# First mixer: 31-tap convolution moved to TensorE strips; first expert stage: pipeline in a written-out order, overflow branch at its head

## The chip, the cores and the metric

One Trainium2 chip, one of its cores. The kernel is one launch. The metric is device time in microseconds (us) of that launch. Beside it stands a profile of one execution, with a trace of every instruction: TensorE (PE, and PEld for its weight loads), VectorE (DVE), ScalarE (ACT), GpSimd (POOL) and SyncE's DMA queue (SP).

## The reference, cut to what matters

Two layers over 256 latent and 256 context tokens of 1024 channels. The parts that this change touches:

```python
def conformer_conv(p, dw_w, dw_b, ln_g, ln_b):
    v, g = jnp.split(p, 2, -1)
    u = v * jax.nn.sigmoid(g)
    u = depthwise_conv(u, dw_w, PAD_A) + dw_b          # 31 taps along the tokens, 512 channels
    return jax.nn.silu(layer_norm(u, ln_g, ln_b))

def moe(h, router_w, router_bias, w_gate, w_up, w_down):   # 16 experts, each token goes to two
    ...
    for e in range(N_EXPERTS):
        hid = jax.nn.silu(t @ w_gate[e]) * (t @ w_up[e])
        out = out + combine[:, e:e + 1] * (hid @ w_down[e])
    return out.reshape(shp)
```

The first layer's mixer runs `conformer_conv` beside a bidirectional gated recurrence (RG-LRU) and one output projection; both layers end in `moe`, the first over 512 tokens, the second over the 256 latent tokens.

## The kernel before

All matrix products keep fp32 accuracy by splitting each operand into a rounded part and its rest (`hi`, `lo`, both fp32r) and adding three products. A weight arrives from DRAM as a 1 MB tile `raw` (SP issues it), is split in two halves by ACT (line 138, `hi`) and DVE or POOL (line 140, `lo`) into a pair of `hl` tiles, and is used by PE. `Feeder` keeps that going: `load` issues transfers into free tiles, `one` splits one half, `get` hands out the next pair. There are four pairs; three `raw` tiles always, and more (`rawx`, `rawy`) in the expert stages.

The order of instructions on an engine is set by a scheduler that follows dependencies and priorities, except inside `in_order()`, where the order of the program text is the order on PE, ACT, DVE and POOL.

**First mixer** (lines 560 to 815). Channels lie on partitions, four groups g of 128; tokens run along the free axis, both segments side by side (512 columns). `value_gate(g)` projects the value and gate columns and writes the gated product into the padded buffer `ups` (line 607). The depthwise convolution goes by `taps`: for every one of 31 taps one instruction over 128x512 multiplies by the channel's weight and adds into `u2` (line 625 on DVE, lines 622 and 623 on POOL). Group 3 is POOL's, groups 2, 1 and 15 taps of group 0 are DVE's, and 16 taps of group 0 are PE's with a diagonal matrix for each tap (`taps_pe`, line 639). Between them stand the recurrence's small convolution (`ub` to `vl`, lines 661 to 668), its gates on PE (line 680), coefficients and scans, the projections for `gg`, and the modulation products with the conditioning vector (`ada_fill`; line 350: four products of 128x32 by 512 columns in the four column strips of the array). A layer norm over channels follows; its first product is line 906, after which `u2` is centred (line 913).

**First expert stage** (`moe`, lines 1121 to 1310). For each expert, a matrix `pm` picks its up to 128 tokens; an indirect DMA on POOL gathers them (`xg`, line 1144), PE transposes them (line 1165), ACT and DVE split them into `xT`. Then gate and up (24 products of 128x128 by 512 columns each, line 1177), `silu(gate)*up` (lines 1240 and 1242), four transposes (1245), a split (1246, 1247), down (24 products, line 1271), a weighted copy into `y` (1276 on ACT, 1277 on DVE) and a scatter to `YD` on POOL (1157). The last two experts are not scattered but combined by products with a placing matrix (line 1305). Before expert 14 stands `overflow` (line 1015): a branch that is taken only when more than 128 tokens chose one expert. There too the rows of `YD` are read back, and four weight tiles (`HOLD`) are held back until then. The second expert stage (`moe_latent`) is written inside `in_order()` and is not changed.

Of the kernel before, what the change touches and what calls it, by code (L numbers as in the profile page):

```python
# [14 lines left out]
D = 1024  # L15
# [32 lines left out]
HOLD = 4  # L48
# [120 lines left out]
def _body(tc, nc, pool, psum, dram, a):  # L169
# [89 lines left out]
    V.memset(PRb[:, :128], 0.0)  # L259

    def late_params():
# [9 lines left out]
        Q.dma_start(PRb[:124, 128:256], a["a_dw_w"].rearrange("o t (k p) -> (o t k) p", p=128))  # L271
        Q.dma_start(PRb[:12, 256:384], a["c_conv_w"].rearrange("o t (k p) -> (o t k) p", p=128))
# [139 lines left out]
    DWT = pool.tile([128, 136], F32, name="DWT")  # L412
# [112 lines left out]
    for g in (2, 1):  # L525
        vg_unit(g)
    half_unit(2)
    vg_unit(0)
# [26 lines left out]
    T.transpose(pp[:, 128:252], PRb[:124, 128:256], ident[:124, :124])  # L555
    T.transpose(pp[:, 252:264], PRb[:12, 256:384], ident[:12, :12])
    V.tensor_copy(PRT[:, 48:128], pp[:, :80])
    V.tensor_copy(DWT, pp[:, 128:264])
    cmR, PR_ = open_pool("mix0_right", "right")
    feed.ada = (PR_, RAWM0)  # L560
# [38 lines left out]
    ups_ = [ups[:, 576 * g:576 * g + 572].rearrange("p (s t) -> p s t", s=2) for g in range(4)]  # L599
# [12 lines left out]
    def taps(g, eng, ts):  # L612

        dst = seg(u2[:, 512 * g:512 * g + 512])
        for t in ts:
            w = DWT[:, 4 * t + g:4 * t + g + 1]
            src = ups_[g][:, :, t:t + 256]
            if t == 0:
                ins = eng.tensor_scalar(dst, src, w, param("a_dw_b", g), OP.mult, OP.add)
            elif eng is G:  # L620
                m_ = seg(PR_.tile([128, 512], F32, name="cm", tag="cm", bufs=1))
                G.tensor_tensor(m_, src, w.unsqueeze(2).broadcast_to([128, 2, 256]), OP.mult)
                ins = G.tensor_tensor(dst, dst, m_, OP.add)
            else:
                ins = V.scalar_tensor_tensor(dst, src, w, dst, OP.mult, OP.add)  # L625
        if len(ts):
            mark(f"conv{g}", ins)

    def taps_pe(g, ts):
        pt = bank()  # L630
        diag = PR_.tile([128, 2048], F32, name="diag", tag="iv", bufs=1)
        for n, t in enumerate(ts):
            d_ = diag[:, 128 * n:128 * n + 128]
            w = DWT[:, 4 * t + g:4 * t + g + 1]
            if DIAG(n):
                S.activation(d_, ident, AF.Copy, scale=w)
            else:
                G.tensor_tensor(d_, ident, w.broadcast_to([128, 128]), OP.mult)
            T.matmul(seg(pt), d_, ups_[g][:, :, t:t + 256], start=n == 0, stop=n == len(ts) - 1)
        return pt  # L640
# [66 lines left out]
    def lru(d):  # L707
        if d:
            load_gates(1)
        lru_gates(d)  # L710
        lru_coeff(d)
        lru_scan(d)

    feed.pool_lo = PL_S
    lru(0)
    value_gate(0)
    lru(1)
    gg = PR_.tile([128, 2048], F32, name="gg", tag="vl", bufs=1)
    for g in range(4):
        pt = proj(nT, feed.get())  # L720
        S.activation(gg[:, 512 * g:512 * g + 512], pt, AF.Gelu_apprx_tanh)
        ada_fill(ADA_E)
    def row_bc(A, third, j0, r, nh):
# [12 lines left out]
    def add_experts(layer, u0, u1):  # L736
        us = []
        for e in range(NE):
            units = []
            for nm in ("moe_w_gate", "moe_w_up"):  # L740
                w = a[nm][layer, e].rearrange("(p k) f -> p k f", p=128)
                units += [(w[:, k0:k0 + 4], 512) for k0 in (0, 4)]
            w = a["moe_w_down"][layer, e].rearrange("(p k) n -> p k n", p=128)
            units += [(w[:, k0:k0 + 2], 1024) for k0 in (0, 2)]
            us += units
        for u in us[u0:u1]:
            feed.add(*u)
# [44 lines left out]

    taps(3, G, range(31))
    taps(0, G, range(POOL_TAPS))
    for g in (2, 1):
        taps(g, V, range(31))
# [6 lines left out]
    pt = taps_pe(0, range(31 - PE_TAPS, 31))  # L803
    taps(0, V, range(POOL_TAPS, 31 - PE_TAPS))
    dst = seg(u2[:, :512])
    V.tensor_tensor(dst, dst, seg(pt), OP.add)
# [315 lines left out]
    def moe(layer, nt, pl, before_tail=None):  # L1122
# [28 lines left out]
        def dispatch(e):  # L1151
            pd = pick(e, slots(e), 0, 8)
            gather(e, pd)
            weight(e, pd)

# [14 lines left out]
        def unit(out_, s, wp, k0, m, last):  # L1170
            hi, lo = wp
            for k in range(2):
# [3 lines left out]
                for l, r_ in ((xh, wh), (xh, wl), (xl, wh)):  # L1176
                    ins = T.matmul(out_, l, r_, start=m == 0, stop=m == last)  # L1177
                    if m == 0:
                        mark("e%d" % e, ins)
# [8 lines left out]
        for e in range(2):  # L1188
            first.append(slots(e))
            gather(e, pick(e, first[e], 0, 4))  # L1190
            if e == 1:

                V.tensor_scalar(one, disp[:, 1, 0:1], 0.0, 1.0, OP.mult, OP.add)
                feed.gate, feed.boost = one, GBOOST
                feed.split()
                feed.gate, feed.boost = None, BOOST
# [20 lines left out]
        s = xT(0)  # L1217
        for e in range(NE):
            if e == NE - 4:
                zero = pl.tile([128, D], F32, name="zero", tag="y", bufs=3)  # L1220
                G.memset(zero, 0.0)
            if e == NE - 2:

                overflow(layer, nt, pl, posm)
                yss = [feed.raw_tile(True) for _ in range(nt)]
                for i in range(nt):
                    Q.dma_start(yss[i], YD[256 * i:256 * i + 256].rearrange("(p t) d -> p (t d)", t=2))
                add_experts(layer, 6 * NE - HOLD, 6 * NE)
                feed.load()
            pgu = []  # L1230
            for _ in range(2):
                pb = bank()
                pgu.append(pb)
                m = 0
                for k0 in (0, 2, 4, 6):
                    m = unit(pb, s, feed.get(), k0, m, 23)
            if e < NE - 1:
                sn = xT(e + 1)
            sl_ = tmp()
            S.activation(sl_, pgu[0], AF.Silu)  # L1240
            hd = tmp()
            V.tensor_tensor(hd, sl_, pgu[1], OP.mult)
# [5 lines left out]
            if e + 2 < NE:  # L1248
                dispatch(e + 2)
                if e + 2 >= NE - 2:  # L1250
                    scatter(e + 2, zero)
            if e == NE - 1:
                gbs = [pl.tile([128, D], F32, name="gb", tag="xg", bufs=2) for _ in range(nt // 2)]
                for r in range(nt // 2):
                    for nh in range(2):
                        S.activation(gbs[r][:, 512 * nh:512 * nh + 512], row_bc(A, 2, 2, r, nh), AF.Copy)
                for i in range(nt):
                    ys = yss[i]
                    G.tensor_tensor(ys[:, :D], ys[:, :D], ys[:, D:], OP.add)
# [653 lines left out]
```

## Time and profile before

| | |
|---|---|
| median of 3 runs | 1280.6 us (1279.28 to 1281.32) |
| the profiled execution's own time | 1279.8 us |
| its span, first to last instruction | 1278.1 us |
| PE busy | 1099.0 us, 86% |
| DVE busy | 991.4 us, 78% |
| ACT busy | 718.4 us, 56% |
| POOL busy | 459.5 us, 36% |
| mean granted TensorE clock | 0.940 |
| moved by DMA | 303.46 MB, 237 GB/s |

Busy time is a sum over stages that differ. The span falls into: norm and modulation (to 58), first mixer (58 to 236), its output projection and routing (236 to 324), first expert stage (324 to 678), second mixer (to about 870) and second expert stage (to the end).

### The profile page before, as it was taken

To read this page: it belongs to the slowest core of one execution; us is meant where nothing else is said; L and a number is where in the kernel's file an instruction comes from. 1 tells how busy PE (TensorE), PEld (TensorE's weight loads), DVE (VectorE), ACT (ScalarE), POOL (GpSimd) and SP (SyncE) were. 2 spreads that over 40 slices of the span, in tenths; PEclk is the share of its full clock that TensorE was granted. 3 is DMA by queue.
4 is the path that set the end of the run, shared out by engine and by line. 5 is a ranking of instruction groups with operands and counts; after the bars stand their busy time and mean duration, and the time that the engine had idled before them with its cause. 6 is when DMAs were issued, how large, how long until landed. Compare 5 with 4: busy or idle time off the path is not lost. (4 is left out here: it accounts for less than half of the span.)

```text
span 1278.1 us, 15407 instructions
## 1 busy us (share of the span) xinstructions
PE 1099.0 (86%) x5370; PEld 823.1 (64%) x5371; DVE 991.4 (78%) x1210; ACT 718.4 (56%) x962; POOL 459.5 (36%) x393
## 2 busy tenths in 40 slices
PE   5896479897799999999888999996699888898975
PEld 3664245585577777777666866665577677776763
DVE  3369999856799999898895335775988888879983
ACT  4321455423577777777664234452578667768781
POOL 3299912444111121212414500023345445545551
PEclk9898689998799999999997999998899999999997
DMA  9772217431699989999595477732678877878840
GB/s 302 233 253 93 82 66 282 193 119 66 254 313 330 344 315 332 332 362 331 198 361 183 150 265 271 256 149 82 202 262 295 295 279 268 298 268 312 288 180 33
DMA packets 94063, 303.46 MB, mean 237 GB/s; under 512 B 14930, under 2 KB 56161, under 8 KB 64792
## 3 DMA queue, kind: packets, MB, share of 16 engines
q1 hardware_dynamic: 89160, 293.38, 64.8%
q0 software_dynamic: 4816, 9.00, 2.2%
q8 instruction: 45, 0.74, 0.2%
q14 instruction: 42, 0.34, 0.1%
HBM read 299.15 MB, written 11.60 MB: 243 GB/s over the span
## 5 line engine op out<-in xcount | busy, mean ns | idle before, releaser
L140 DVE TENSOR_TENSOR hl<-rawx,hl 128x1024 fp32r<-128x1024 f32 x163 | 226.5, 1396 | 28.3 <-ACT hl L138 24.5
L140 DVE TENSOR_TENSOR hl<-raw,hl 128x1024 fp32r<-128x1024 f32 x128 | 175.5, 1380 | 68.4 <-ACT hl L138 50.0
L138 ACT ACTIVATE hl<-rawx 128x1024 fp32r<-128x1024 f32 x174 | 182.3, 1059 | 66.1 <-PE psa L1271 22.9
L138 ACT ACTIVATE hl<-raw 128x1024 fp32r<-128x1024 f32 x142 | 148.7, 1057 | 123.2 <-PE psb L453 30.9
L1509 PE MATMUL psa<-hl,xT 128*128 128x512 f32 x432 | 118.6, 422 | 21.3 <-DVE xT L1589 17.1
L1509 PE MATMUL psa<-hlx,xT 128*128 128x512 f32 x432 | 116.9, 417 | 12.4 <-DVE xT L1589 10.2
L1509 PEld LDWEIGHTS psa<-hl,xT 128*128 128x128 f32 x432 | 85.1, 201 | 45.2 <-DVE xT L1589 12.9
L1509 PEld LDWEIGHTS psa<-hlx,xT 128*128 128x128 f32 x432 | 84.4, 200 | 36.2 <-DVE xT L1589 9.1
L1144 POOL DMA_INDIRECT xg<-XN,dispi x16 | 29.4, 1840 | 192.2 <-DVE pm L1131 168.3
L1177 PE MATMUL psb<-hl,xT 128*128 128x512 f32 x384 | 93.9, 400 | 0.4 <-PEq L1017 0.4
L1271 PE MATMUL psb<-hl,xT 128*128 128x512 f32 x192 | 81.1, 422 | 13.6 <-ACT xT L1246 9.6
L1177 PE MATMUL psa<-hl,xT 128*128 128x512 f32 x384 | 92.2, 396 | 0.0
L1177 PEld LDWEIGHTS psb<-hl,xT 128*128 128x128 f32 x384 | 72.6, 190 | 18.6 <-issue 0.8
L1177 PEld LDWEIGHTS psa<-hl,xT 128*128 128x128 f32 x384 | 72.1, 188 | 17.5
L1271 PE MATMUL psa<-hl,xT 128*128 128x512 f32 x192 | 78.0, 406 | 2.9 <-DVE xT L1247 2.2
L453 PE MATMUL psb<-nT,hl 128*128 128x512 f32 x288 | 76.6, 413 | 0.1
L625 DVE SCALAR_TENSOR_TENSOR u<-ups,DWT,u 128x512 f32<-128x512 f32 x74 | 76.2, 1071 | 0.2
L453 PEld LDWEIGHTS psb<-nT,hl 128*128 128x128 f32 x288 | 55.1, 195 | 20.7 <-issue 5.6
L140 DVE TENSOR_TENSOR hlx<-rawx,hlx 128x1024 fp32r<-128x1024 f32 x38 | 59.9, 1586 | 7.5 <-ACT hlx L138 7.3
L140 POOL TENSOR_TENSOR hlx<-rawx,hlx 128x1024 fp32r<-128x1024 f32 x18 | 49.2, 2733 | 45.6 <-ACT hlx L138 40.8
L140 POOL TENSOR_TENSOR hl<-raw,hl 128x1024 fp32r<-128x1024 f32 x14 | 38.0, 2716 | 62.5 <-ACT hl L138 60.3
L140 POOL TENSOR_TENSOR hl<-rawx,hl 128x1024 fp32r<-128x1024 f32 x17 | 45.4, 2671 | 39.5 <-ACT hl L138 32.3
(501 smaller groups left out, 2335.9 us busy)
## 6 DMA issues: line engine op xcount, KB each, us to landing
rawx<-in_moe_w_down_dram SPq DMA_DIRECT2D x40, 1024.0 KB
rawx<-in_moe_w_gate_dram SPq DMA_DIRECT2D x39, 1024.0 KB
rawx<-in_moe_w_up_dram SPq DMA_DIRECT2D x37, 1024.0 KB
raw<-in_ada_w_dram SPq DMA_DIRECT2D x24, 1024.0 KB
raw<-in_moe_w_up_dram SPq DMA_DIRECT2D x24, 1024.0 KB
raw<-in_moe_w_gate_dram SPq DMA_DIRECT2D x23, 1024.0 KB
raw<-in_moe_w_down_dram SPq DMA_DIRECT2D x20, 1024.0 KB
rawx<-in_ada_w_dram SPq DMA_DIRECT2D x16, 1024.0 KB
```

What stands on the lines that cost most here:

```text
L138: nc.scalar.activation(h3, src, AF.Copy, scale=1.0 if self.gate is None else self.gate)
L140: (nc.gpsimd if self.pool_lo and self.ns % self.pool_lo == 0 else nc.vector).tensor_tensor(l3, src, h3.bitcast(F32), OP.subtract)
L453: ins = T.matmul(pt, l, r, start=k == 0 and m == 0, stop=k == 7 and m == 2)
L625: ins = V.scalar_tensor_tensor(dst, src, w, dst, OP.mult, OP.add)
L1144: G.indirect_dma_start(out=xgs[e % 2], out_offset=None, in_=XN, in_offset=bass.IndirectOffsetOnAxis(ap=dispi[:, e, 1:2], axis=0), bounds_c ...
L1177: ins = T.matmul(out_, l, r_, start=m == 0, stop=m == last)
L1271: T.matmul(pb, l, w_[:, 512 * nh:512 * nh + 512], start=m == 0, stop=m == 11)
L1509: ins = T.matmul(po, l, w_[:, c0:c0 + 512], start=k == 0 and m == 0, stop=k == n * per - 1 and m == len(mm) - 1)
```

## The change

**Convolution.** `taps` and `taps_pe` go. `pack(g)` makes a tile `cz` in which partition 32j+c holds channel c of a strip of 32 channels shifted by j tokens, for the four strips of group g: 16 transfers from `ups`, issued by POOL. `conv(g)` builds two weight tiles on POOL and runs 8 times 4 products (K = 4 taps x 32 channels, 32 columns out, 512 tokens), one for each strip of the array; ACT adds the bias on the way to `u2`. There is one `cz` buffer. `value_gate`, `lru_gates`, `lru_coeff` and `lru_scan` are written in another order, the weight tiles likewise, and the separate tile for the modulation weights (`rawm`) goes, so these share the three `raw` tiles.

**First expert stage.** It runs inside `in_order()`: up of expert e+1 stands between gate and down of expert e, split into halves around the four transposes; the transposes for `xT` of expert e+2 come after down; splits (`split()`) are placed by hand between the products; both halves of `y` are ACT's. The overflow branch moves ahead of the first split tiles. `HOLD` is 0. The read-back of `YD` comes after expert 14, and its additions are placed among expert 15's products.

```diff
@@ first mixer
-    feed.ada = (PR_, RAWM0)
+    zs = {}
+    def pack(g):
+        z = zs[g] = PR_.tile([128, 4, 2, 288], F32, name="cz", tag="cz", bufs=1)
+        for G4 in range(4):
+            for j in range(4):
+                G.dma_start(z[32 * j:32 * j + 32, G4, :, :284], ups_[g][32 * G4:32 * G4 + 32, :, j:j + 284])
+    def conv(g):
+        ws = []
+        for h in range(2):
+            ws.append(tmp().rearrange("p (q G c) -> p q G c", q=8, c=32))
+            G.tensor_tensor(ws[-1], gsum.unsqueeze(1).unsqueeze(1).broadcast_to([128, 8, 2, 32]),
...
+        for q in range(8):
+            for G4 in range(4):
+                T.matmul(seg(pt[32 * G4:32 * G4 + 32]), ws[G4 // 2][:, q, G4 % 2], zs[g][:, G4, :, 4 * q:4 * q + 256],
+                         start=q == 0, stop=q == 7)
+        S.activation(u2[:, 512 * g:512 * g + 512], pt, AF.Identity, bias=param("a_dw_b", g))
...
     value_gate(3, early.pts)
-    for g in (2, 1):
-        value_gate(g)
+    pack(3)
     for g in range(4):
         pt = proj(nT, feed.get())
         if g == 0:
             load_gates(0)
+        if g == 2:
+            conv(3)
...
-    lru(0)
+    lru_gates(0)
+    value_gate(2)
+    pack(2)
+    lru_coeff(0)
+    value_gate(1)
+    conv(2)
+    pack(1)
+    lru_scan(0)
+    load_gates(1)
+    lru_gates(1)
     value_gate(0)
-    lru(1)
+    conv(1)
+    pack(0)
+    lru_coeff(1)
+    lru_scan(1)
...
-    taps(3, G, range(31))
-    taps(0, G, range(POOL_TAPS))
-    for g in (2, 1):
-        taps(g, V, range(31))
...
-    pt = taps_pe(0, range(31 - PE_TAPS, 31))
-    taps(0, V, range(POOL_TAPS, 31 - PE_TAPS))
@@ first expert stage
+        overflow(layer, nt, pl, posm)
+        V.tensor_scalar(one, disp[:, 1, 0:1], 0.0, 1.0, OP.mult, OP.add)
+        feed.gate, feed.boost = one, GBOOST
+        feed.split()
...
+        def expert(e):
+            s = ops[e]
+            if e + 2 < NE:
+                pms[e + 2] = slots(e + 2)
+            pg, m = bank(), 0
+            for k0 in (0, 2, 4, 6):
+                m = product(pg, e, k0, m)
+                if k0 < 6:
+                    split()
+                    rest(1)
...
+            if e + 1 < NE:
+                pu, m = bank(), 0
+                for k0 in (0, 2):
+                    m = product(pu, e + 1, k0, m)
+                    split()
             ph = bank()
             for k in range(4):
                 T.transpose(ph[:, 128 * k:128 * k + 128], hd[:, k::4], ident)
...
+                for k0 in (4, 6):
+                    m = product(pu, e + 1, k0, m)
+                    split()
...
-                V.tensor_scalar(y[:, 512:], pd1, w_, None, OP.mult)
+                S.activation(y[:, 512:], pd1, AF.Copy, scale=w_)
                 scatter(e, y)
...
+            split()
+            if e + 2 < NE:
+                ops[e + 2] = xT(e + 2)
```

What this does to the order on the engines, at the places that the prediction speaks of.

PE, second half of the first mixer, before (`nT,hl` projections, `vl,gw` gates of the recurrence, `condT` modulation, `ups,diag` taps, `Am` the broadcast of gates ahead of line 906):

```order
L453 MATMUL psb<-nT,hl 128x512 x16
L639 MATMUL psa<-ups,diag 128x512 x2
L350 MATMUL psa<-raw,condT 32x512 x4
L639 MATMUL psa<-ups,diag 128x512 x3
L350 MATMUL psa<-rawm,condT 32x512 x4
L639 MATMUL psa<-ups,diag 128x512 x11
L727 MATMUL psb<-Am_92,ident 128x512
```

and PE with the change, from the end of `value_gate(1)` to the start of `conv(0)` (`cz,tmp` are the strips):

```order
L353 MATMUL psa<-raw,condT 32x512 x4
L678 MATMUL psb<-vl,gw 128x512 x4
L456 MATMUL psb<-nT,hl 128x512 x5
L635 MATMUL psa<-cz,tmp 32x512 x3
L678 MATMUL psa<-vl,gw 128x512
L635 MATMUL psa<-cz,tmp 32x512 x29
L678 MATMUL psa<-vl,gw 128x512 x3
L456 MATMUL psb<-nT,hl 128x512 x19
L353 MATMUL psa<-raw,condT 32x512 x4
L456 MATMUL psa<-nT,hl 128x512 x24
L353 MATMUL psa<-raw,condT 32x512 x4
L456 MATMUL psa<-nT,hl 128x512 x3
```

The taps on PE, which stood at the end, are replaced by four blocks of 32 strip products that stand among projections and gates; the next row after this piece is the first strip product of `conv(1)`.

POOL in the same stretch, with the change, from the end of the recurrence's constants (`NSP`) to the sums for the layer norm (line 902):

```order
L585 TENSOR_SCALAR NSP_480<-w_481 128x8
L622 DMA cz<-ups 32x2x284 x16
L629 TENSOR_TENSOR tmp<-gsum,DWT 128x512 x2
L622 DMA cz<-ups 32x2x284 x16
L629 TENSOR_TENSOR tmp<-gsum,DWT 128x512 x4
L902 TENSOR_TENSOR tmp<-u_513 128x512
L622 DMA cz<-ups 32x2x284 x16
L902 TENSOR_TENSOR tmp<-tmp,u_513 128x512 x2
```

Before, 30 pairs of a multiply and an add over 128x512 stood here; now there are the packs of groups 2, 1 and 0, the last one behind a layer-norm sum. The pack of group 3 stands ahead, mixed one to one with the small instructions of the recurrence's constants.

PE, an expert in the middle of the first expert stage, with the change (`pm` the pick for expert e+2, `ident,tmp` the four transposes):

```order
L1157 MATMUL psb<-ident,xg 128x128 x4
L1157 MATMUL psa<-ident,xg 128x128 x4
L1169 MATMUL psb<-hl,xT 128x512 x24
L1135 LDWEIGHTS pm
L1135 MATMUL psa<-RM,pm 128x8
```

```order
L1135 MATMUL psa<-RM,pm 128x8
L1169 MATMUL psb<-hl,xT 128x512 x12
L1251 MATMUL psa<-ident,tmp 128x128 x4
L1169 MATMUL psb<-hl,xT 128x512 x12
L1266 MATMUL psb<-hl,xT 128x512
```

The first piece is gate of expert e, with the operand of the expert after it just before; the second is up of expert e+1, cut in half by the transposes of expert e, and then down of expert e. Before, gate and up of one expert stood together, and the transposes and down followed them with nothing between.

## Rows read from the trace of the kernel before

**Rows 1.** Busy time by stretch; columns as in the second line.

```profile
core 0: us, PE busy (x) PEld busy (x) DVE busy (x) ACT busy (x) POOL busy (x), PEclk, DMA share, GB/s
58.50:236.00 177.50, 139.58 (x538) 80.90 (x537) 162.12 (x163) 70.78 (x102) 114.48 (x98) 0.88 0.42 148
...
352.73:597.96 245.23, 228.41 (x1057) 181.60 (x1056) 220.78 (x253) 182.96 (x205) 41.20 (x26) 1.00 0.93 334
...
928.00:1216.00 288.00, 257.24 (x1295) 210.72 (x1294) 250.18 (x222) 207.72 (x250) 141.92 (x52) 0.97 0.81 285
```

**Rows 2.** Groups by line, 58.5 to 236: busy, mean ns | idle before, releasers.

```profile
L625 DVE SCALAR_TENSOR_TENSOR u<-ups,DWT,u 128x512 f32<-128x512 f32 x74 | 76.2, 1071 | 0.2
...
L680 PE MATMUL psb<-vl,gw 128*128 128x512 f32 x16 | 12.5, 876 | 32.8 <-DVE vl L668 26.8 <-DVE ups L607 5.4 <-PE psa L453 0.6
```

**Rows 3.** Timeline of PE, first mixer: start, us, instruction [idle before <-releaser].

```profile
70.58 1.06 PE L350 MATMUL psa<-raw,condT 128*32 128x512 f32 x8
...
94.70 5.76 PE L453 MATMUL psa<-nT,hl 128*128 128x512 f32 x24
100.30 5.76 PE L453 MATMUL psb<-nT,hl 128*128 128x512 f32 x24
...
124.99 2.04 PE L680 MATMUL psb<-vl,gw 128*128 128x512 f32 x2 [10.80 <-DVE vl L668]
...
168.49 1.02 PE L680 MATMUL psb<-vl,gw 128*128 128x512 f32 x2
...
236.26 1.55 PE L906 MATMUL psb<-tmp,onesm 128*128 128x512 f32 x2 [2.64 <-POOL tmp L905]
```

**Rows 4.** Timeline of DVE, the centring of the layer norm.

```profile
240.04 2.47 DVE L913 TENSOR_TENSOR u<-u,psb 128x512 f32<-128x512 f32 x4
```

**Rows 5.** Timelines of POOL, and of DVE at 471.40: transfers that POOL issues, a split beside one.

```profile
344.17 0.99 POOL L1144 DMA_INDIRECT xg<-XN,dispi  x1 [21.98 <-DVE pm L1131]
...
471.40 1.23 DVE L140 TENSOR_TENSOR hl<-raw,hl 128x1024 fp32r<-128x1024 f32 x1
...
471.54 1.98 POOL L1144 DMA_INDIRECT xg<-XN,dispi  x1 [13.30 <-DVE pm L1131]
...
705.28 0.68 POOL L1689 DMA_DIRECT2D tmp<-in_d_rpb_dram  x1
...
709.55 0.55 POOL L1691 DMA_DIRECT2D RP<-tmp  x1 [0.34 <-DVE tmp L1690]
```

**Rows 6.** DMA issues: size, median us from issue to landing.

```profile
RP<-tmp POOLq DMA_DIRECT2D x1, 60.0 KB, 1.9
```

**Rows 7.** Timeline of ACT, first mixer: the one wait for a weight tile.

```profile
83.12 1.06 ACT L138 ACTIVATE hl<-raw 128x1024 fp32r<-128x1024 f32 x1 [2.64 <-DMA raw<-in_ab_w_in_dram]
```

**Rows 8.** Timeline of PE, an expert in the middle of the first stage.

```profile
385.92 0.74 PE L1245 MATMUL psb<-ident,tmp 128*128 128x128 f32 x4 [0.41 <-DVE tmp L1242]
387.35 0.50 PE L1271 MATMUL psb<-hl,xT 128*128 128x512 f32 x1 [0.69 <-ACT xT L1246]
...
388.85 0.50 PE L1271 MATMUL psb<-hl,xT 128*128 128x512 f32 x1 [0.31 <-DVE xT L1247]
```

**Rows 9.** Timeline of PE, start and end of the first expert stage.

```profile
324.00 1.12 PE L1165 MATMUL psb<-ident,xg 128*128 128x128 f32 x4 [3.48 <-DMA xg<-XN,dispi]
...
636.58 0.80 PE L1271 MATMUL psa<-hl,xT 128*128 128x512 f32 x1 [2.20 <-DVE xT L1247]
...
663.89 0.63 PE L1305 MATMUL psb<-yy,tmp 128*128 128x512 f32 x2
...
671.22 0.79 PE L1305 MATMUL psa<-yy,tmp 128*128 128x512 f32 x1 [2.19 <-DVE yt L1288]
...
678.29 1.07 PE L425 MATMUL psb<-rawx,condT 128*32 128x256 f32 x16
```

**Rows 10.** Timeline of PE, the first products after each overflow branch.

```profile
618.92 5.84 PE L1177 MATMUL psb<-hl,xT 128*128 128x512 f32 x24 [0.37 <-PEq L1017]
...
1244.45 3.75 PE L1509 MATMUL psa<-hl,xT 128*128 128x512 f32 x8 [3.88 <-DVEq L1017]
```

More of the change, by code (lines that the diff above doesn't have):

```diff
@@ L47 @@
 RP_POS = 1
-HOLD = 4
+HOLD = 0
 ADA_PRE = 3
@@ L610, in _body @@
     u2 = PW.tile([128, 2048], F32, name="u2", tag="u2", bufs=1)
[L612 to L627, printed above, removed]
@@ L722, in _body @@
         ada_fill(ADA_E)
+        if g == 1:
+            conv(0)
     def row_bc(A, third, j0, r, nh):
@@ L736, in add_experts @@
     def add_experts(layer, u0, u1):
+        parts = [("up", 0)]
+        for e in range(NE):
+            parts += [("gate", e)] + [("up", e + 1)] * (e + 1 < NE) + [("down", e)]
         us = []
[L738 to L745, printed above, removed]
+        for part, e in parts:
+            w = a["moe_w_" + part][layer, e].rearrange("(p k) f -> p k f", p=128)
+            step = 2 if part == "down" else 4
+            us += [(w[:, k0:k0 + step], 2048 // step) for k0 in (0, step)]
         for u in us[u0:u1]:
@@ L1216, in moe @@
             weight(e, pick(e, first[e], 4, 8))
[L1217 to L1242, printed above, removed]
+        overflow(layer, nt, pl, posm)
@@ new lines, in moe, with split, rest, product @@
+        V.tensor_scalar(one, disp[:, 1, 0:1], 0.0, 1.0, OP.mult, OP.add)
+        feed.gate, feed.boost = one, GBOOST
+        feed.split()
+        feed.gate, feed.boost = None, BOOST
+        feed.ahead = 1
+        ops, pus, pms = {}, {}, {}
+        later = deque()
+        def split(n=1):
+            for _ in range(n):
+                feed.one()
+        def rest(n):
+            for _ in range(n):
+                if later:
+                    later.popleft()()
+        def product(pb, e, k0, m):
+            return unit(pb, ops[e], feed.get(), k0, m, 23)
@@ L1272, in moe @@
                     m += 1
+                if kk < 3:
+                    split()
+                    rest(2)
+            rest(99)
             w_ = disp[:, e, 2:3]
@@ L1289, in moe, with add @@
                 last.append(yy)
-            s = sn
+            split()
+            if e + 2 < NE:
+                ops[e + 2] = xT(e + 2)
+        zeros = []
+        with in_order():
+            ops[0] = xT(0)
+            pus[0], m = bank(), 0
+            for k0 in (0, 2, 4, 6):
+                m = product(pus[0], 0, k0, m)
+                split()
+            ops[1] = xT(1)
+            for e in range(NE - 2):
+                if e == NE - 4:
+                    zeros.append(pl.tile([128, D], F32, name="zero", tag="y", bufs=3))
+                    G.memset(zeros[0], 0.0)
+                expert(e)
+        gbs = [pl.tile([128, D], F32, name="gb", tag="xg", bufs=2) for _ in range(nt // 2)]
+        with in_order():
+            expert(NE - 2)
+            yss = [feed.raw_tile(True) for _ in range(nt)]
+            for i in range(nt):
+                Q.dma_start(yss[i], YD[256 * i:256 * i + 256].rearrange("(p t) d -> p (t d)", t=2))
+            if before_tail:
+                before_tail()
+            for r in range(nt // 2):
+                for nh in range(2):
+                    S.activation(gbs[r][:, 512 * nh:512 * nh + 512], row_bc(A, 2, 2, r, nh), AF.Copy)
+            def add(i, st):
+                ys = yss[i]
+                if st == 0:
+                    G.tensor_tensor(ys[:, :D], ys[:, :D], ys[:, D:], OP.add)
+                elif st == 1:
+                    V.tensor_tensor(ys[:, :D], ys[:, :D], gbs[i // 2], OP.mult)
+                else:
+                    V.tensor_tensor(Hi(i), Hi(i), ys[:, :D], OP.add)
+            for i in range(nt):
+                add(i, 0)
+            for i in range(nt):
+                for st in (1, 2):
+                    later.append(lambda i=i, st=st: add(i, st))
+            expert(NE - 1)
+        feed.ahead = 3
         PTs = []
```

84 lines of the change are left out of this document (26 added, 58 removed).

## The prediction

> **What bounds the kernel now.** Four views, in this order. First the busy time by stretch [rows 1]: in the first mixer DVE is busy 162.1 of 177.5 us (91%), PE 139.6 (79%) and at a mean granted clock of 0.88; in twelve experts of the first expert stage PE is busy 228.4 of 245.2 us (93%), DVE 90%, DMA 93%. So the mixer hangs on DVE, the experts on PE, with DVE and DMA close behind. Second the groups by line in the mixer [rows 2]: 74 taps are 76.2 us of DVE, and PE's gate products wait 26.8 us for the small convolution that DVE puts out between the taps. Third PE's timeline: one such wait of 10.80 us [rows 3], and at the end the layer norm's first product, 236.26, whose successor on DVE, the centring, starts at 240.04 [rows 4]. Fourth PE within an expert: before the four transposes it stands 0.41 us, before the first down product 0.69, four products later 0.31 [rows 8], 1.41 us in every period of 245.23 / 12 = 20.44 us [rows 1].
>
> The sum is made against the profiled execution's own 1279.8 us; the median is 0.8 above that. A measurement here can tell about 0.2% (2.6 us) from nothing.
>
> **Mixer: the price of the strips.** Taps leave DVE (76.2 us), POOL and PE; 128 strip products come to PE. Four of them, 32 columns wide, are what the modulation products are already: eight records in 70.58 to 71.58, 1.0 us for four strips [rows 3]. Conv of one group is eight such sets, 8.0 us; four groups 32.
>
> PE's whole list from 58.8 on, with nothing missing and at full clock: 14 projections at 5.60 (24 products, 94.70 to 100.30 [rows 3]) = 78.4; 16 modulation sets 16.0; 16 pairs of gate products at 1.02 [rows 3], with their overlap 16.0; conv 32.0; four broadcasts at 1.0, 4.0; transposes 0.8. That is 147.2 and ends at 206.0.
>
> **Mixer: the packs.** There is one `cz`, so the strips of a group can be fetched only when the previous conv is through. POOL issues 16 transfers, one after the other, and PE waits for the last. The landing is put at 2.0 us (a transfer of 60 KB landed 1.9 after issue [rows 6]; these carry about 73 KB). The issue is the disputed price. Plain transfers by POOL took 0.55 and 0.68 us [rows 5]. A gather by POOL took 0.99 where DVE had just finished, and 1.98 where a split of DVE began just ahead of it [rows 5]: a DVE instruction can hold an issue back by its own length. After the change DVE works some 86 us (162.1 - 76.2) in about 155, so a transfer meets an instruction 0.55 of the time and would lose about half of 1 us: 0.68 + 0.28 = 0.96. No row shows that a plain transfer suffers so. I take 0.82, midway between 0.68 and 0.96; the ends are 0.55 and 1.98.
>
> At 0.68 a pack is 10.9 + 2.0 = 12.9 us, and the order of PE gives what covers it:
> - pack(3) stands one to one between the constants' small instructions on POOL (estimated at 0.18 each): begun at about 65.9, when group 3 is gated, it ends at 65.9 + 13.8 + 2.0 = 81.7. PE gets to conv(3) after 72 products (16.8), two modulation sets, transposes and some 0.7 lost, at 79.1. Stall 2.6.
> - pack(2) begins when value_gate(2) is gated; PE has value_gate(1), modulation and the second half's gates until conv(2), some 18 us less 1.5 for gating: slack 3.9.
> - pack(1) waits for conv(2); PE has gates, 1.8 projections and two modulation sets: slack 1.7.
> - pack(0) waits for conv(1) and for a layer-norm sum on POOL ahead of it, with 12 us of PE work beside it: stall 2.6.
>
> At 0.82 each pack is 2.2 longer: stalls 4.8, 0, 0.5, 4.8. After a stall PE runs slower: behind the 2.20 us gap at 636.58 the product shows 0.80 instead of 0.50 [rows 8, 9]; 1.3 us after each of two stalls, 2.6. The modulation weights now share the three `raw` tiles with the projections; the one wait on a weight tile was 2.64 [rows 7], and I count one more, 2.6. Together 15.3, so the layer norm's first product stands at 206.0 + 15.3 = 221.3, 15.0 earlier. DVE has no taps left at that point, so the centring follows at once rather than 3.8 us behind [rows 3, 4]; 3.0 more. Mixer: 18.0.
>
> **First expert stage.** It reaches from 324.00 to 678.29 [rows 9], 354.3 us. On the times of before (all shift alike with the mixer):
> - Start. The branch at the head costs something that the middle no longer pays: the first product after a branch came 0.37 us late in one place, 3.88 in the other [rows 10]. I take 1.5. Then the transposes and splits of two experts 1.8 and 0.9, and up of expert 0 alone, 5.6 and 1.5 for the slow clock after the 3.48 us wait: 335.3.
> - 14 experts. The waits of 1.41 us lie behind half of up (2.8 us of products) in the new order: 20.44 - 1.41 = 19.03. I allow 0.5 for new ones (the fixed order lets no ready product pass), 19.5; 273 in all: 608.3. DMA would then be busy 0.93 x 20.44 / 19.5 = 0.975 of the time [rows 1]; it holds, with the tiles loaded ahead as reserve, but barely. DVE loses half of `y`, 0.75 an expert, to ACT, which has room (183 of 245).
> - Expert 14 has no operand to prepare, 17.4, with 3.4 of broadcasts from the next stage: 629.1. Expert 15 has no up of a successor between: gate 5.6, `silu` and its product uncovered 2.2, transposes 0.6, split 0.7, down 5.6, and 0.5 as above, 15.2: 644.3.
> - Combining took 14.4 (663.89 to 678.29), with a wait of 2.19 on DVE and products at the slow pace behind it [rows 9]. Its 32 products at the pace of the first pair (0.63 with overlap, 0.46 from start to start) are 7.4; with the additions placed by hand I take 9.5. End 653.8.
>
> The stage gains 24.5. `HOLD` 0 costs nothing as long as the read-back of `YD` finds tiles; the four loads were only held back, not added.
>
> **Sum:** 18.0 + 24.5 = 42.5; 1279.8 - 42.5 = 1237.3, **1237 us**.
>
> **Rivals.**
> - *DMA holds the expert's period.* If the transfers cannot be denser than 0.93, the period stays 20.44, and 14 x 0.94 = 13 us are lost: 1250. For it: 334 GB/s over twelve experts without a gap. Against it: PE, not a transfer, ends the waits there [rows 8]. Chance 0.15.
> - *The fixed order brings its own waits.* The second expert stage is written out in the same way, and there PE is busy only 257.2 of 288 us, 0.893 [rows 1]. An expert of 19.03 us of work would take 21.3: 14 x 1.8 = 25 lost, 1262. Against it: that stage has half the tokens, so its products give less cover for a split. Chance 0.10.
> - *The packs are slower than what they replace.* The place is POOL's queue: if each of the 64 issues is held back like the gather [rows 5], 1.98 instead of 0.68 adds 1.30 x 64 - 5.6 (the two slacks) = 77.6 to the 1232 that the sum gives at 0.68: 1310. The point from which it decides is 64d - 5.6 = 47.5, d = 0.83, an issue of 1.5 us. For it: the gather shown took twice its time beside a split, and DVE in the mixer runs the splits, gates and scans. Against it: the two plain transfers [rows 5], and DVE is idle more than four tenths of the mixer without taps. Chance 0.12 that an issue takes over 1.2 us (64 x 0.52 - 5.6 = 28 and more, 1260 and up), half of it beyond 1280.
>
> By the Trainium skill, "SBUF — State Buffer", section "SBUF: two separate sides", a transfer issued by POOL has its descriptors written through a port that DVE can lock, and takes some 3100 ns instead of 620 beside certain DVE copies. The row at 1.98 beside 0.99 [rows 5] agrees in kind; no row here shows it for a plain transfer. As an estimate from that page's figure alone, 64 x 2.42 - 5.6 = 149 us would be added, 1381.
>
> - *Better.* Issues of 0.55, no stalls, no new waits in the experts: 1237 - 15 - 7 = 1215.
>
> **How the numbers follow.** Forecast 0.55 (its own range 1217 to 1250), DMA 0.15, fixed order 0.10, slow packs 0.12, better 0.08. The range runs from 1215 to 1266: it takes in the better end, the first two rivals and slow packs up to about 1.3 us, and leaves out some 2 in 10. Slower by over 0.2%: half of slow packs, 0.06, and 0.04 for several rivals together. Within 0.2%: 0.02. Faster: 0.88.
>
> **What the profile will show.** Right: strip groups of 1.0 us for four; POOL's pack instructions at 0.7 to 1.0; PE's waits on `cz` ahead of conv(3) and conv(0) only, some 5 us each; the layer norm's first product near 221; mean clock in the mixer near 1.00; a period of 19 to 19.5 us per expert with no wait on `tmp` or `xT` above 0.2; the stage 330 us long. Wrong: pack instructions over 1.2; waits on `cz` at all four convs; strips that run one after another (2 us and more for four); PE waits on `hl` with DMA named as releaser in the experts; a longer second expert stage, which nothing here should touch.

## The result, and the profile after

| | before | changed |
|---|---|---|
| median of 4 runs | 1279.94 us (1274.27 to 1281.32) | 1240.28 us (1236.13 to 1253.20) |
| ratio to before, 95% interval | | 0.9715 [0.9635, 0.9796] |
| the profiled execution, its span | 1279.8, 1278.1 | 1236.1, 1234.4 |

1237 was forecast. The changed kernel spreads more than the kernel before, and its profiled execution is its fastest, so what follows is a trace of the lower end; a second one is among the experiments.

The busy time by stretch, first the mixer up to the layer norm, then some 12.7 experts of the first stage, columns as in [rows 1]:

```profile
58.00:215.25 157.25, 151.36 (x759) 82.57 (x758) 67.95 (x84) 71.71 (x100) 56.84 (x102) 0.98 0.60 185
329.69:574.00 244.31, 236.99 (x1128) 189.73 (x1129) 220.38 (x259) 199.75 (x231) 33.47 (x29) 1.00 0.96 357
```

DVE has gone from 91% of the mixer to 43%, PE from 79% to 96%, and the mean clock from 0.88 to 0.98. In the experts PE went from 93% to 97%, DMA from 0.93 to 0.96. The timeline of PE through the mixer, which answers to [rows 3]:

```profile
67.35 0.73 PE L456 MATMUL psb<-nT,hl 128*128 128x512 f32 x2 [1.68 <-ACT hl L138]
70.69 4.86 PE L456 MATMUL psb<-nT,hl 128*128 128x512 f32 x14 [2.61 <-DVE hl L140]
...
85.34 7.07 PE L635 MATMUL psa<-cz,tmp 128*32 128x512 f32 x64
92.34 5.86 PE L456 MATMUL psb<-nT,hl 128*128 128x512 f32 x24
...
140.72 7.05 PE L635 MATMUL psa<-cz,tmp 128*32 128x512 f32 x58
...
165.23 7.05 PE L635 MATMUL psb<-cz,tmp 128*32 128x512 f32 x58
...
215.25 1.02 PE L903 MATMUL psa<-tmp,onesm 128*128 128x512 f32 x2
```

No strip product waits for `cz`. A whole group takes 85.34 to 92.34, 7.0 us, 0.875 for four strips. The layer norm's first product stands at 215.25 instead of 236.26, 21.0 earlier. POOL's timeline shows why nothing waits, and one thing that was not foreseen:

```profile
122.73 4.30 POOL L622 DMA_DIRECT2D cz<-ups  x8 [40.72 <-DVE th L689]
129.40 3.68 POOL L622 DMA_DIRECT2D cz<-ups  x7 [2.37 <-DMA cz<-ups]
...
148.08 7.93 POOL L622 DMA_DIRECT2D cz<-ups  x15 [12.19 <-PE psa L635]
...
173.70 8.45 POOL L622 DMA_DIRECT2D cz<-ups  x16
```

An issue takes 0.53 us. In the pack at 122.73, and only there, POOL waits after eight of them until one of the earlier transfers has landed; the packs at 148.08 and 173.70 issue 15 and 16 in a row. The three stretches, columns as in [rows 1], and a split of DVE's that stood in the last of them:

```profile
122.73:133.80 11.07, 11.07 (x54) 7.00 (x53) 10.04 (x16) 6.93 (x10) 8.51 (x16) 1.00 1.03 314
148.08:156.71 8.63, 8.63 (x37) 5.16 (x36) 2.73 (x4) 4.61 (x6) 8.46 (x16) 1.00 0.52 125
173.70:182.15 8.45, 8.45 (x41) 5.90 (x40) 7.58 (x10) 2.94 (x3) 8.44 (x17) 1.00 0.67 181
```

```profile
179.47 1.21 DVE L140 TENSOR_TENSOR hl<-raw,hl 128x1024 fp32r<-128x1024 f32 x1
```

The pack that waited is the one with the DMA engines full, at a share of 1.03; the median landing of its transfers took 5.7 us, against 2.2 and 3.5 in the other two. Over all four packs the landing took, by the view of the tile `cz`,

```profile
DMA to landing us min/median/max: 1.9/4.3/6.9
```

PE in the first expert stage, which answers to [rows 8, 9]:

```profile
301.63 1.09 PE L1157 MATMUL psa<-ident,xg 128*128 128x128 f32 x4 [4.48 <-PEq L1014]
...
310.98 5.84 PE L1169 MATMUL psb<-hl,xT 128*128 128x512 f32 x24
...
350.20 0.71 PE L1157 MATMUL psb<-ident,xg 128*128 128x128 f32 x4 [1.89 <-DMA xg<-XN,dispi]
...
580.60 5.84 PE L1169 MATMUL psb<-hl,xT 128*128 128x512 f32 x24
...
594.64 0.50 PE L1266 MATMUL psa<-hl,xT 128*128 128x512 f32 x1 [1.19 <-DVE xT L1253]
...
600.68 0.50 PE L1266 MATMUL psa<-hl,xT 128*128 128x512 f32 x1 [1.66 <-DVE hl L140]
...
606.93 5.87 PE L1169 MATMUL psa<-hl,xT 128*128 128x512 f32 x24 [1.61 <-DVE yy L1287]
617.14 1.10 PE L1251 MATMUL psb<-ident,tmp 128*128 128x128 f32 x4 [4.34 <-DVE tmp L1236]
...
626.55 0.62 PE L1349 MATMUL psa<-yy,tmp 128*128 128x512 f32 x2
...
634.20 1.07 PE L428 MATMUL psa<-rawx,condT 128*32 128x256 f32 x16
```

The stage is 332.6 us long (301.63 to 634.20) instead of 354.3. From the gate of expert 0 (310.98) to that of expert 14 (580.60) it is 14 periods of 19.26 us. The three waits of [rows 8] are gone; in their place PE waits for the rows that POOL gathers, as the list of its waits from 310 to 590 has it (us in total, times, longest):

```profile
PE psb L1157 <- DMA xg<-XN,dispi: 9.3, 8, 2.0
```

Behind the stage both spans run on for about as long, 600.2 us here and 599.8 before, though by differences that cancel (last section).

### The profile page after: what moved, and what is told of

Its sections match the earlier page's. It is cut to its first block, busy times and chain, and to the rows that moved or that the text cites. A ratio compares the mean times of both kernels' runs of the same rounds, so it can differ in the third digit from the quotient of the medians.

```text
span 1234.4 us, 15863 instructions
## 1 busy us (share of the span) xinstructions
PE 1091.7 (88%) x5595; PEld 812.2 (66%) x5596; DVE 884.6 (72%) x1118; ACT 724.8 (59%) x973; POOL 389.4 (32%) x396
## 5 line engine op out<-in xcount | busy, mean ns | idle before, releaser
L1169 PE MATMUL psb<-hl,xT 128*128 128x512 f32 x696 | 172.1, 400 | 0.0
L1169 PEld LDWEIGHTS psb<-hl,xT 128*128 128x128 f32 x696 | 127.7, 188 | 27.4
L1553 PE MATMUL psa<-hl,xT 128*128 128x512 f32 x432 | 116.6, 417 | 15.8 <-DVE xT L1633 15.0
L1553 PEld LDWEIGHTS psa<-hl,xT 128*128 128x128 f32 x432 | 84.4, 200 | 39.4 <-DVE xT L1633 13.0
L1266 PE MATMUL psa<-hl,xT 128*128 128x512 f32 x192 | 77.6, 404 | 3.7 <-DVE hl L140 1.7
L1266 PE MATMUL psb<-hl,xT 128*128 128x512 f32 x192 | 77.3, 403 | 0.1
L456 PE MATMUL psa<-nT,hl 128*128 128x512 f32 x264 | 69.6, 408 | 4.7 <-POOL nT L490 2.5
L456 PEld LDWEIGHTS psa<-nT,hl 128*128 128x128 f32 x264 | 48.6, 189 | 28.6 <-issue 6.9
L1141 POOL DMA_INDIRECT xg<-XN,dispi x16 | 21.5, 1341 | 141.9 <-PE psa L1251 68.7
L456 PE MATMUL psb<-nT,hl 128*128 128x512 f32 x216 | 58.1, 415 | 4.8 <-DVE hl L140 2.6
L138 ACT ACTIVATE hlx<-rawx 128x1024 fp32r<-128x1024 f32 x54 | 55.5, 1055 | 4.9 <-PE psa L1553 4.8
L456 PEld LDWEIGHTS psb<-nT,hl 128*128 128x128 f32 x216 | 41.5, 196 | 20.0 <-issue 4.2
```

Source lines behind the costliest of these rows:

```text
L138: nc.scalar.activation(h3, src, AF.Copy, scale=1.0 if self.gate is None else self.gate)
L456: ins = T.matmul(pt, l, r, start=k == 0 and m == 0, stop=k == 7 and m == 2)
L1141: G.indirect_dma_start(out=xgs[e % 2], out_offset=None, in_=XN, in_offset=bass.IndirectOffsetOnAxis(ap=dispi[:, e, 1:2], axis=0), bounds_c ...
L1266: T.matmul(pb, l, w_[:, 512 * nh:512 * nh + 512], start=m == 0, stop=m == 11)
L1553: ins = T.matmul(po, l, w_[:, c0:c0 + 512], start=k == 0 and m == 0, stop=k == n * per - 1 and m == len(mm) - 1)
```

## The experiments

**The changed kernel again, and its two halves.** One kernel has the convolution with the expert stage of before (`moe`, `add_experts` and `HOLD` = 4 taken back), the other the new expert stage behind the taps of before.

```diff
@@ convolution alone
-HOLD = 0
+HOLD = 4
-    def add_experts, def moe of the changed kernel
+    def add_experts, def moe of the kernel before
@@ experts alone: the kernel before, with
-HOLD = 4
+HOLD = 0
-    def add_experts, def moe of the kernel before
+    def add_experts, def moe of the changed kernel
```

> The changed kernel as it is, to see how far its own executions spread. Its four so far lie between 1236.1 and 1253.2 us at a granted clock of 0.949 to 0.961, those of the kernel before between 1274.3 and 1281.3. If the spread comes from the new expert stage, whose gathered rows land just when PE wants them (waits of 0.5 to 2.0 us in the profiled execution, 9.3 in all), another execution shows other waits at the same lines. If it comes from the chip, the same waits and another clock. Median 1236 to 1245.

> The convolution's half of the change alone, with the expert stage of before. Theory (the halves add): the expert stage starts 22.4 us earlier, as in the changed kernel, and takes its 354.3 us: 1280 - 22 = 1258. Rival (the stage gives it back, as its first weight tiles have less time to come in before it): 1264 to 1272, with waits of the splits on weight tiles in the first experts.

> The expert stage's half alone, with the taps of before. Theory (the halves add): the stage takes 332.6 us instead of 354.3, 1280 - 22 = 1258. Rival (the stage is held by DMA, whose share is 0.96 in it; the later start gives more tiles ahead): shorter waits on gathered rows, 1250 to 1254.

Measured against 1275.23 for the kernel before: the change 1241.43 (1235.94 to 1246.09), ratio 0.9726 [0.9681, 0.9770]; convolution alone 1261.67, 0.9884 [0.9852, 0.9915]; experts alone 1259.24, 0.9867 [0.9840, 0.9894]. The savings of 1.16% and 1.33% add to 2.49%, against 2.74% together: the halves add, within the intervals. What the new order of the mixer gives and what the strips give was not run apart, nor were the parts of the new expert stage. In the traces the first product of the stage and the first behind it are, for the convolution alone,

```profile
302.51 1.12 PE L1163 MATMUL psa<-ident,xg 128*128 128x128 f32 x4 [3.33 <-DMA xg<-XN,dispi]
...
656.63 1.07 PE L428 MATMUL psa<-rawx,condT 128*32 128x256 f32 x16
```

and for the experts alone

```profile
328.01 1.09 PE L1159 MATMUL psb<-ident,xg 128*128 128x128 f32 x4 [4.57 <-PEq L1016]
...
666.09 1.07 PE L425 MATMUL psb<-rawx,condT 128*32 128x256 f32 x16
```

That is 354.1 us for the stage of before, 21.5 us earlier, as the theory had it: the stage gives nothing back. The time still fell by 13.6 us only and not by 22, since 606.6 us follow the stage in that trace and 599.8 before. The new stage behind the old mixer takes 338.1. In the second trace of the change,

```profile
299.92 1.09 PE L1157 MATMUL psa<-ident,xg 128*128 128x128 f32 x4 [4.20 <-PEq L1014]
...
636.03 1.07 PE L428 MATMUL psa<-rawx,condT 128*32 128x256 f32 x16
```

the stage takes 336.1, with waits on gathered rows of 10.3 us, and 606.7 us follow it. So the new stage took 332.6 to 338.1 us in three executions; the rest of the spread lies behind it (last section).

**Packs of twice the transfers.**

```diff
-                G.dma_start(z[32 * j:32 * j + 32, G4, :, :284], ups_[g][32 * G4:32 * G4 + 32, :, j:j + 284])
+                for s_ in range(2):
+                    G.dma_start(z[32 * j:32 * j + 32, G4, s_, :284], ups_[g][32 * G4:32 * G4 + 32, s_, j:j + 284])
```

> Every transfer of a pack in two halves, one for each segment: 32 issues of some 0.53 us instead of 16. A pack gets 8.5 us longer. Theory (POOL's queue decides once the cover is gone): the cover in the changed kernel is what lies between the landing and the first strip product, about 4.0, 2.9, 4.9 and 1.3 us for groups 3, 2, 1 and 0, so PE waits 4.5 + 5.6 + 3.6 + 7.2 = 21 us, 1261. Rival (the transfers overlap so far that the issue is not what decides, only bytes): under 1246.

Measured: 1274.92 us, ratio 0.9993 [0.9964, 1.0023], all of the change's gain gone, some 14 us more than the theory's 1261. POOL and PE, at the pack and the strips of group 2, and the layer norm's first product:

```profile
135.89 3.92 POOL L623 DMA_DIRECT2D cz<-ups  x8 [44.44 <-DVE ups L610]
140.97 3.92 POOL L623 DMA_DIRECT2D cz<-ups  x8 [1.16 <-DMA cz<-ups]
147.41 3.92 POOL L623 DMA_DIRECT2D cz<-ups  x8 [2.52 <-DMA cz<-ups]
...
159.35 2.07 POOL L630 TENSOR_TENSOR tmp<-gsum,DWT 128x512 f32<-128x512 f32 x2
```

```profile
160.48 2.92 PE L636 MATMUL psa<-cz,tmp 128*32 128x512 f32 x6 [7.16 <-POOL tmp L630]
...
247.28 1.02 PE L904 MATMUL psa<-tmp,onesm 128*128 128x512 f32 x2
```

PE's waits before strips come to 20.8 us in five places; the sum is as expected (21), the places are not (6.8, 7.2, 2.5 and 4.4 us for groups 3, 2, 1 and 0). The norm's product moves by 32.0, to 11 us later than in the kernel before: the mean clock up to there is 0.91 instead of 0.98, which the expectation had left out. PE is busy 163.7 us instead of 151.4 up to there. And the wait is not for the strips alone: the strips' weights are made by POOL behind the pack, at 159.35, and the longest wait, 7.16, is for them. The rival on the other side is hereby a real one: POOL's queue has cover for one pack of 16 and not for twice that.

**The gather.** In two runs the pick and the gather for expert e+2 were moved ahead: to the middle of gate, and to three quarters of it. The diff is of the second, the first has `k0 == 2`.

```diff
             for k0 in (0, 2, 4, 6):
                 m = product(pg, e, k0, m)
+                if k0 == 4 and e + 2 < NE:
+                    pd = pick(e + 2, pms.pop(e + 2), 0, 8)
+                    gather(e + 2, pd)
+                    weight(e + 2, pd)
+                    if e + 2 >= NE - 2:
+                        scatter(e + 2, zeros[0])
...
             split()
-            if e + 2 < NE:
-                pd = pick(e + 2, pms.pop(e + 2), 0, 8)
...
```

> The pick and the gather for expert e+2 move from behind gate and two splits of expert e into the middle of gate. In the changed kernel the gather was issued some 4 us after its pick, behind two splits on DVE (pick 336.29, issue 340.43), and the rows landed 0.5 to 2.0 us after PE wanted them, in 8 of 13 experts. Theory (the late gather is what keeps the period at 19.3 instead of 18.6): issue some 4 us earlier, no waits on the gathered rows, 9 to 10 us less: 1231. Rival (the transfers of weights, busy 0.96 of the time, then set the period): waits on weight tiles or splits come in its place, 1237 to 1242.

Measured: 1248.69, ratio 0.9791 [0.9765, 0.9816], some 8 us slower than the change and not 9 faster. Neither theory nor rival had it. PE's waits from 300 to 640:

```profile
PE psa L1135 <- DVE pm L1128: 19.1, 14, 1.5
```

No wait on gathered rows is left in that list, but the matrix `pm` was late, which DVE makes behind the splits of the operand: waits of 9 us were traded for waits of 19. Hence the second one:

> The pick and gather for expert e+2 at three quarters of gate instead of behind it. In the run with the pick at half of gate the waits on gathered rows were gone, but PE waited 19.1 us in 14 places (1.4 each) for the matrix that picks, which DVE makes behind the last split of an operand; at three quarters, 1.4 us of products later, that matrix is just there. Theory (the late gather and nothing else costs some 10 us): waits for it 3 us at most in all, the gather issued 3 us earlier than in the changed kernel, waits on its rows under 2 us in all; 1233. Rival (whatever is taken from one wait comes back as another, PE's products being held by splits and transfers): 1238 to 1245.

Measured: 1233.62 (1228.10 to 1237.62), ratio 0.9648 [0.9622, 0.9673], below the interval of the change in its second measurement. The stretch of experts, and two issues of the gather in a row:

```profile
330.00:570.00 240.00, 239.44 (x1129) 190.44 (x1128) 220.80 (x260) 199.01 (x232) 33.16 (x29) 1.00 0.96 364
```

```profile
336.41 1.33 POOL L1141 DMA_INDIRECT xg<-XN,dispi  x1 [6.02 <-PE psb L1169]
...
355.14 1.33 POOL L1141 DMA_INDIRECT xg<-XN,dispi  x1 [6.02 <-PE psb L1169]
```

PE is busy 239.4 of 240 us, the period 18.73, and DMA moves 364 GB/s at a share of 0.96. So transfers did not hold the period of 19.26; the late gather did. This version beats both kernels.

**Half of `y` on DVE again.**

```diff
-                S.activation(y[:, 512:], pd1, AF.Copy, scale=w_)
+                V.tensor_scalar(y[:, 512:], pd1, w_, None, OP.mult)
```

> The second half of each expert's result is copied by DVE again, as before the change, 0.75 us an expert. DVE was busy 0.90 of the middle experts in the changed kernel, ACT 0.82. Theory (DVE has that much slack, PE sets the period): 0 to 3 us more, 1241 to 1244. Rival (DVE's queue is in the chain through the late gather, which stands behind its splits): the period grows by 0.3 to 0.75, 4 to 10 us more, 1245 to 1251.

Measured: 1240.15, ratio 0.9724 [0.9692, 0.9755], no change that the time shows. DVE has slack for its half of `y`.

**The read-back's additions.** Leaving them out:

```diff
-            for i in range(nt):
-                add(i, 0)
```

> Leaves out part of the computation: the addition of the two contributions that each read-back row carries (four instructions on POOL, 128x1024). In the changed kernel they run at 590 to 602 us, and the splits of DVE beside them take 2.3 us instead of 1.14 (five in 11.71); PE waits 1.19 and 1.66 for a split and 1.61 and 4.34 behind them. Theory (POOL's additions slow the splits): splits at 1.14, the first three waits gone, 4 to 6 us less, 1236. Rival (the late weight tiles of the last experts are behind those waits): no change.

Measured: 1231.41, ratio 0.9655 [0.9628, 0.9683], some 9 us less; the stage is 327.1 us long. DVE's splits in the last down but one, with POOL's additions beside them (the changed kernel) and without:

```profile
594.50 11.71 DVE L140 TENSOR_TENSOR hl<-rawx,hl 128x1024 fp32r<-128x1024 f32 x5
```

```profile
589.51 3.51 DVE L140 TENSOR_TENSOR hl<-rawx,hl 128x1024 fp32r<-128x1024 f32 x3
```

2.34 us each against 1.17, and the waits of 1.19, 1.66 and 1.61 are gone; the wait of 4.34 in expert 15 stays. What cannot be left out can be put elsewhere. Three tries: DVE's own additions out of expert 15's gate; besides that, POOL's held back until that gate is done; and that with the gather at three quarters.

```diff
-                    rest(1)
-            rest(99)
...
                 last.append(yy)
+                rest(99)
@@ held back, in the second and third
             V.tensor_tensor(hd, sl_, pus.pop(e), OP.mult)
+            if e == NE - 1:
+                G.tensor_scalar(held, hd[:, 0:1], 0.0, 1.0, OP.mult, OP.add)
+                for i in range(nt):
+                    add(i, 0)
```

> The read-back's multiplications and additions on DVE leave the gate of expert 15 (three of them) and the end of its down products; what is left of them after down comes behind the split of its result. In the changed kernel PE waits 4.34 us for the product of gate and up of expert 15, which stands behind one of them on DVE. Theory: that wait falls to 2, with 1 us of slow clock behind it, 3 us less, 1238; what is left over at the end of the stage gives back at most 2. Rival (what is moved simply waits at the end): no change within 2 us.

> Nothing is left out. The four additions on POOL are held back until DVE has made the product of gate and up of expert 15 (a small instruction on POOL that reads it stands ahead of them), the multiplications and additions on DVE stand among the down products and behind the split of the result. Theory (the additions cost by slowing DVE's splits, which end before that point): as in the run that left them out, splits of 1.14 us during expert 14, the stage about 327 us long instead of 332 to 336, less 3 us for the wait on that product, plus up to 3 at the end: 1231 to 1235. Rival (they then stand in the chain to the end of the stage): 1238 to 1244.

> The gather at three quarters of gate and the held-back additions together. If both theories hold the gains add, 1240 - 8 - 8 = 1224, and this beats the changed kernel; if the one or the other rival holds, 1231 to 1236.

Measured: 1240.12, 0.9715 [0.9688, 0.9742]; 1241.66, 0.9716 [0.9688, 0.9745]; 1231.29, 0.9643 [0.9616, 0.9671]. The first cut the wait on the product of gate and up from 4.3 to 1.5 us, with no gain that the time shows. In the second and third, holding back gave nothing either, alone or with the gather: PE now waited 5.7 and 6.7 us for a placing matrix, which DVE made behind a multiplication that waited for POOL. The last run made those matrices earlier:

```diff
             V.tensor_tensor(s[:, 1024:1536], ph, s[:, 0:512].bitcast(F32), OP.subtract)
+            if e == NE - 1:
+                place(NE - 2)
+                place(NE - 1)
```

> The gather at three quarters of gate and the held-back additions, and the two placing matrices of the last experts made by DVE right after the split of expert 15's hidden rows, ahead of everything that waits for POOL's additions. In the run without this last step PE waited 6.7 us for a placing matrix, which stood on DVE behind a multiplication that waited for POOL. Theory (that place in DVE's order is what ate the gain of the held-back additions): the wait goes, the stage gets 5 to 7 us shorter than 324.9, of which the additions on DVE that then end last let some 3 come through: 1228. Rival (DVE's additions end the stage in either case, the next norm waits for them): 1230 to 1234, as with the gather alone.

Measured: 1239.38, ratio 0.9724 [0.9701, 0.9747], 0.8% slower than without that step. The stage is 324.6 us long in its trace, not 318; without the step it was 324.9. The trace without the step is of an execution of 1236.97 us, one of its slower ones, so the two traces do not show where the 0.8% lies, and its cause stays open. DVE and POOL:

```profile
604.85 7.21 DVE L1230 TENSOR_SCALAR tmp<-iota,dcol 128x128 fp32r<-128x128 f32 x4
...
612.24 0.87 DVE L1230 TENSOR_SCALAR tmp<-iota,dcol 128x128 fp32r<-128x128 f32 x4
```

```profile
601.47 5.67 POOL L1338 TENSOR_TENSOR raw<-raw 128x1024 f32<-128x1024 f32 x2
607.10 2.39 POOL L1338 TENSOR_TENSOR rawy<-rawy 128x1024 f32<-128x1024 f32 x1
609.45 2.34 POOL L1338 TENSOR_TENSOR rawx<-rawx 128x1024 f32<-128x1024 f32 x1
```

The same four instructions take 7.21 us while POOL adds, 1.80 each beside additions of 2.3 to 2.8, and 0.87 together just after. So it is not only the splits that POOL's additions slow. PE then waited 3.5 us for a placing matrix and 4.6 for DVE's weighted result, and 8.8 before the second mixer's norm (6.2 in the second trace of the change). What the additions cost in the place that the change gives them is shown, some 9 us; a better place for them was not found.

## Why the prediction was right, point by point

The total was right (1237 for 1240.3, and 42.5 us for the 43.7 between the two spans), while its terms erred in both directions.

That it came so near is partly luck. The mixer and the expert stage together gain 44.1 us in the first trace of the change (22.4 and 21.7) and 42.3 in the second (24.1 and 18.2), as forecast. But what follows them, which the prediction took as unchanged, is 600.2 us in the one and 606.7 in the other, against 599.8 before. In the first trace PE's wait at the last overflow branch was 0.5 and not 3.9 us (last section); the rest of the difference is open. In the second measurement, with thirteen executions of the kernel before, the medians lie 33.8 us apart and not 42.5.

| step | forecast | in the trace |
|---|---|---|
| four strips at once | 1.0 us | 0.875 |
| an issue by POOL, its landing | 0.82, 2.0 us | 0.53 to 0.6 (the first 0.81), 4.3 |
| waits for strips | 4.8, 0, 0.5, 4.8 us | none |
| layer norm's first product | 221.3 | 215.25 |
| gain to the start of the stage | 18.0 | 22.4 |
| period of an expert | 19.5 us | 19.26 |
| expert 14, expert 15, combining | 20.8, 15.2, 9.5 us | 26.3, 19.6, 7.7 |
| the stage | 329.8 us | 332.6, 336.1 again |

- **What bounds.** DVE's taps set the mixer, and with them gone PE does, at 0.98 of its clock: right.
- **Packs.** The step that failed is "I take 0.82". Between 122.73 and 133.80 DVE was busy 10.0 of 11.1 us and an issue still took 0.53, and so did the issues beside the split at 179.47: plain transfers were not held back by DVE's work there, as the gather of [rows 5] was. The rule of the Trainium skill that the prediction weighed ("SBUF — State Buffer", section "SBUF: two separate sides", a transfer issued by POOL slowed beside certain DVE copies) does not show in these rows; DVE ran operations on two operands and scans then, and no run here has its copies beside a pack. The split of [rows 5] is an operation on two operands too and no copy, so that row is not a case of the rule, though the prediction says that it agrees in kind. Landings took longer than the 2.0 put in, 4.3 in the middle, which gave part of that back. The other half of the miss is the cover: PE came to conv(3) at 85.34 and not at 79.1, as it had waited 4.3 us for split tiles at 67 and 71, and so the pack was there. (The other wait that was put in, 2.6 us for a tile of modulation weights, came to 1.1 in two places.) With d = 0.53 for doubled issues the prediction's line 64d - 5.6 gives 28; the packs of 32 cost 32.0 at the norm. That nearness is luck: the packs' cover was about 13.1 us (the expectation of that run) and not 5.6, so that only 20.8 of the 32.0 are waits; the rest came with the lower clock, which the line leaves out.
- **PE's list in the mixer.** 147.2 us, less 4.0 for the cheaper strips, against 151.4 busy: 8.2 short. 2.8 of it is that a projection with another kind of block behind it takes 5.80 and not 5.60 (112.76 to 118.56 with a modulation set of 1.0 between two); the rest is open.
- **Centring.** From the norm's product to the stage it is 86.4 us instead of 87.7: 1.4 gained of the 3.0. The branch at the head stands in that stretch. With the convolution alone, and no branch there, it is 86.3 us, so that the branch costs 0.1; with the experts alone it is 90.6 against 87.7, 2.8. The 1.5 put in for the branch lies between.
- **The experts.** The 1.41 us of [rows 8] went as forecast. PE's own work came out shorter, 18.7 us (236.99 over 12.7 periods of 19.26) for 19.03, 0.3 of it since three entries that stood behind waits in [rows 8] got shorter: the transposes (0.74, now 0.63) and two products (0.50, now 0.40). The "0.5 for new ones" was the right size (0.6) and had no name: it is the gather, whose index stands behind two splits in the fixed order on DVE.
- **The rivals.** DMA did not hold the period: 364 GB/s were had with the gather at three quarters. The fixed order did bring its own waits, 9 to 10 us in the middle instead of 25. Slow packs did not come, but would have: at twice the issues the gain is gone.
- **The end of the stage.** Mis-sized by 5.5 and 4.4 us for experts 14 and 15. Beside these two experts the prediction costed the read-back's additions at nothing, without naming a cover. Those on POOL slow DVE's splits to half, and PE waits 1.19, 1.66 and 1.61 us around expert 14. In expert 15 PE waits 4.34 for a product behind DVE's own additions; cutting that to 1.5 gained no time.

## What to carry to other kernels

When a step is moved into a fixed order, follow what it issues through every queue behind it: here the index of a gather, two splits late on DVE, was the whole new wait, and moving it too far ahead put a longer wait in its place. Work "on an idle engine" is not free if it slows a busy engine's instructions: look for a changed duration of unchanged instructions beside it. And judge a forecast by its terms, on more than one execution: a right total can be two wrong ones, or a lucky trace.

## What the runs showed of the hardware that was not expected

- **POOL and DVE.** Beside POOL's additions of two operands DVE's splits took 2.34 us instead of 1.17, and DVE operations of 0.2 us took 1.8. The Trainium skill ("SBUF — State Buffer", section "SBUF: two separate sides") has it that DVE and GpSimd share a pair of ports which one of them holds for a whole instruction, for DVE's two-operand work and its faster modes; the splits, which read two operands, agree with it; whether the operations of 0.2 us ran in a faster mode no row shows.
- **Plain transfers by POOL** cost it 0.53 us. With the DMA engines full (share 1.03) it waited after eight in a row for a landing, 2.37 us at 129.40; at shares of 0.52 and 0.67 it issued 15 and 16 in a row. In the packs of 32 such waits came in every pack (1.16 and 2.52 us in the lines shown).
- **The last overflow branch** costs PE a wait of 0.5 or 3.9 us from one execution to the next, in unchanged code. The changed kernel's two traces:

```profile
1199.99 2.11 PE L1553 MATMUL psa<-hl,xT 128*128 128x512 f32 x8 [0.50 <-DVEq L1014]
```

```profile
1205.57 3.75 PE L1553 MATMUL psa<-hl,xT 128*128 128x512 f32 x8 [3.92 <-DVEq L1014]
```

It was 3.9 in twelve of fourteen traces, and the products behind it start at the slow pace. From the end of the first expert stage to the last product it took 583.6 to 593.2 us in the fourteen, with the same code there.
- **The end of the program.** From DVE's last instruction to the end of the span it is 3.8 us in the kernel before, 3.7 with the experts alone and 3.6 with the packs of 32, but 7.7 in all eleven other traces, the changed kernel's among them, with the same two transfers of 512 KB after it. That takes 3.9 us off the gain. The three are also the three longest spans, 1266.2 us and more against 1263.2 at most in the others; the cause is open.
